# Nearest-neighbour upsampling: which block of rows each partition holds

## The chip, the core and the metric

The kernel runs on one core of a Trainium2 chip. The metric is the device time of one execution in microseconds, the median of several runs. The profile comes from one further execution, whose own time is given beside its span: the time from the first to the last instruction of the core that the profile records.

## The reference

```python
def setup_inputs():
    batch, channels, h, w = (16, 64, 64, 64)
    return {'x': np.random.randn(batch, channels, h, w).astype(np.float32), 'scale_factor': 2}

def reference(x, scale_factor):
    ...
    for i in range(new_h):
        for j in range(new_w):
            src_i = i // scale_factor
            src_j = j // scale_factor
            result[:, :, i, j] = x[:, :, src_i, src_j].copy()
```

Each of 1024 images of 64 x 64 float32 values becomes 128 x 128: every value is repeated twice along its row, and every row twice. 16.78 MB are read and 67.11 MB written.

## The kernel before

The images are taken as 65,536 rows of 64 values (256 B). The rows are cut into 128 blocks of 512 rows, so a block is 128 KiB of `x` and 512 KiB of the output, and partition p of the on-chip memory holds block p (the views `xp` and `op`, lines 173 to 176). In both views the partition is the first dimension and a partition's rows follow one another in DRAM.

One tile, `mem`, holds everything: in each partition a free area of 79 expanded rows first, and then the 512 input rows (`xt`). An expanded row is one input row in its four-fold form, 256 values or 1 KiB.

**Loads.** Line 195 issues four transfers on SyncE (SP), for the rows 0 to 32, 32 to 256, 256 to 480 and 480 to 512 of every partition: 8,192 B, 57,344 B, 57,344 B and 8,192 B per partition. A finalizer, `begin_before_barrier`, moves their issue ahead of the program's opening barrier.

**Groups.** The 512 rows are worked in nine groups of 52, 40, 52, 63, 52, 64, 63, 63 and 63 rows (`rows`, line 181). For each group VectorE (DVE) copies nine sixteenths of the rows with every value and every row repeated (line 215), ScalarE (ACT) the rest (line 216), and SP issues one store of the whole group (line 217): per partition one run of 1 KiB per row, from 40,960 to 65,536 B. Groups with even numbers are expanded into the free area at the tile's start, those with odd numbers into the place just before the end of the input rows that they use up, so the space of two groups is in use at a time. A copy into the free area waits for the store that last read it.

**Order.** All 13 transfers are issued by SP and so stand in one queue in the order of the program. The first store also waits for the third load (the manual dependency of line 219). Of the end, `close_early` makes only what has to wait for the last store wait for it.

A transfer is moved by 16 DMA engines, each of which takes the rows of 8 of the 128 partitions, one packet for a partition's row of bytes, and writes a 4 B semaphore packet behind them: 13 x (128 + 16) = 1872 packets in all.

Of the kernel before, what the change touches and what calls it, by code (L numbers as in the profile page):

```python
# [153 lines left out]
@with_exitstack  # L154
def kernel(
    ctx: ExitStack,
    tc: tile.TileContext,
    x: bass.AP,
    scale_factor: int,
    out: bass.AP,  # L160
):
    nc = tc.nc
    nc.at_finalize(begin_before_barrier)
    nc.at_finalize(close_early)
    P = nc.NUM_PARTITIONS
    s = int(scale_factor)
    B, C, H, W = x.shape
    R = B * C * H // P
    fdt = x.dtype

    xp = x.rearrange("b c h w -> (b c h) w").rearrange("(p r) w -> p r w", p=P)
    op = out.rearrange("b c (h hd) w -> (b c h) (hd w)", hd=s).rearrange(
        "(p r) w -> p r w", p=P
    )

    rows = [52, 40, 52, 63, 52, 64, 63, 63, 63]
    GROW = s * s
    FREE = 79
    WF = FREE * GROW * W
    assert sum(rows) == R
    mem_pool = ctx.enter_context(tc.tile_pool(name="mem", bufs=1))
    mem = mem_pool.tile([P, WF + R * W], fdt, name="mem")
    xt = mem[:, WF:].rearrange("p (r w) -> p r w", r=R)

    HEAD = 32
    cuts = [0, HEAD, R // 2, R - 32, R]
    loads = [
        nc.sync.dma_start(out=xt[:, lo:hi], in_=xp[:, lo:hi])  # L195
        for lo, hi in zip(cuts, cuts[1:])
    ]

    def expanded(r0, r1):
        return (  # L200
            xt[:, r0:r1].unsqueeze(2).unsqueeze(4).to_broadcast([P, r1 - r0, s, W, s])
        )

    r0 = 0
    before = (0, 0)
    for n, k in enumerate(rows):
        size = k * GROW * W
        at = 0 if n % 2 == 0 else WF + r0 * W - size
        assert at >= before[1] or at + size <= before[0]
        before = (at, at + size)  # L210
        u = mem[:, at : at + size].rearrange(
            "p (k a w b) -> p k a w b", k=k, a=s, w=W
        )
        kv = k * 9 // 16
        nc.vector.tensor_copy(out=u[:, :kv], in_=expanded(r0, r0 + kv))  # L215
        nc.scalar.copy(out=u[:, kv:], in_=expanded(r0 + kv, r0 + k))  # L216
        store = nc.sync.dma_start(out=op[:, r0 : r0 + k, :], in_=u)  # L217
        if n == 0:
            tc.add_manual_dep(
                store.ins,  # L220
                loads[-2].ins.name,
                mybir.DependencyInfo(
                    mybir.DependencyClass.Sync, mybir.DependencyReason.DATA
                ),
                reason="stores begin as the loads end",
            )
        r0 += k
# [35 lines left out]
```

## Time and profile before

| | |
|---|---|
| median of 3 runs | 197.2 us (196.95 to 197.35) |
| the profiled execution's own time | 197.0 us |
| its span | 195.7 us |
| DVE busy | 69.7 us (36%), 9 copies, the longest 9.49 us |
| ACT busy | 51.4 us (26%), 9 copies and a table load |
| DMA queue: share of 16 engines' span | 99.3% |
| moved | 83.89 MB, 429 GB/s over the span |
| a load from issue to landing | 4.6 us (the first) to 39.7 us |
| a store from issue to landing | 18.2 to 29.9 us |

A transfer is in a queue from its issue on, so its time to landing holds the time in which earlier transfers of the queue move. The profile's line of DMA tenths cuts the span in 40 slices and gives the busy share of the 16 engines in each, 9 for 90% or more; the line of GB/s gives what they moved, booked where packets end. In the chain of work that ended last, each piece is what released the next one. The trace also records every DMA packet with its size, its start and how long it took, though not which partition or which address it belongs to.

### The profile page before, as it was taken

Reading aid. Unit: us, or ns where it says so; the run is one execution under the profiler, and the core shown is the slowest. Engines: PE = TensorE matmul, PEld = TensorE weight load, DVE = VectorE, ACT = ScalarE, POOL = GpSimd, SP = SyncE. Lnnn points to the kernel's source line nnn. Section 1 sums busy time; section 2 is a strip of 40 time slices with the busy share of each in tenths; the row PEclk is TensorE's granted clock in tenths of the full one; section 3 lists DMA queues with packets and bytes.
Section 4 is the critical chain, followed back from the end, with each engine's and each line's share of the span. In section 5 each row is a group of like instructions: output and inputs, shape, how many; then the busy total and the mean of one; then the engine's idle time right before and its main releaser. Section 6 shows DMA issues by size and latency. Waiting matters only on the chain.

```text
span 195.7 us, 105 instructions
## 1 busy us (share of the span) xinstructions
DVE 69.7 (36%) x9; ACT 51.4 (26%) x10; POOL 0.2 (0%) x4
## 2 busy tenths in 40 slices
DVE  0950600000039299069008205930692079100000
ACT  0000595000036093064910006666000074000000
POOL 0000000000000000000000000000000000000000
DMA  9899889799899989899999899999999999999994
GB/s 402 375 481 457 375 375 563 310 440 523 348 442 452 526 348 512 359 422 422 422 422 523 348 523 429 429 429 429 422 422 422 422 422 422 528 514 422 435 422 211
DMA packets 1872, 83.89 MB, mean 429 GB/s; under 512 B 208, under 2 KB 208, under 8 KB 208
## 3 DMA queue, kind: packets, MB, share of 16 engines
q1 hardware_dynamic: 1872, 83.89, 99.3%
HBM read 16.78 MB, written 67.11 MB: 429 GB/s over the span
## 4 chain that ended last, share of the span: by engine, by line
DMA 67%; DVE 18%; SPq 0%; issue 0%; DVEq 0%
DMA out_dram<-mem 48%; DMA mem<-in_x_dram 19%; DVE mem L215 18%; SPq L195 0%; DVEq L215 0%; SPq L217 0%
## 5 line engine op out<-in xcount | busy, mean ns | idle before, releaser
L215 DVE COPY mem<-mem 128x8960 f32<-128x8960 f32 (+3 forms) x9 | 69.7, 7740 | 97.5 <-DMA out_dram<-mem 83.9
L216 ACT COPY mem<-mem 128x7168 f32<-128x7168 f32 (+2 forms) x9 | 50.1, 5572 | 90.8 <-DMA out_dram<-mem 84.3
L216 ACT ACT_TABLE_LOAD x1 | 1.3, 1283 | 21.6 <-DMA mem<-in_x_dram 21.6
L244 POOL MEMSET const-bfloat16-1.0<- 128x1 bf16 x1 | 0.1, 102 | 0.0
L244 POOL MEMSET const-uint8-127<- 128x1 uint8 x1 | 0.1, 102 | 0.0
L244 POOL MEMSET const-float32-0.0<- 128x1 f32 x1 | 0.1, 99 | 0.2 <-issue 0.2
L244 POOL MEMSET const-float32-1.0<- 128x1 f32 x1 | 0.1, 99 | 0.0
## 6 DMA issues: line engine op xcount, KB each, us to landing
out_dram<-mem SPq DMA_DIRECT2D x4, 8064.0 KB, 28.4
out_dram<-mem SPq DMA_DIRECT2D x3, 6656.0 KB, 19.7
mem<-in_x_dram SPq DMA_DIRECT2D x2, 7168.0 KB, 29.3
out_dram<-mem SPq DMA_DIRECT2D x1, 5120.0 KB, 29.8
mem<-in_x_dram SPq DMA_DIRECT2D x2, 1024.0 KB, 22.1
out_dram<-mem SPq DMA_DIRECT2D x1, 29.9
```

The lines of the kernel that those rows point to most:

```text
L215: nc.vector.tensor_copy(out=u[:, :kv], in_=expanded(r0, r0 + kv))
L216: nc.scalar.copy(out=u[:, kv:], in_=expanded(r0 + kv, r0 + k))
L244: nc = _bacc.Bacc("TRN2", target_bir_lowering=False, num_devices=1)
```

## The change

The view of DRAM is cut in another order. With q from 0 to 7 and a from 0 to 15, partition 8a + q now holds block 16q + a of `x` and of the output, where partition p held block p. Partitions 0 to 7 thus hold the blocks 0, 16, 32, ..., 112, partitions 8 to 15 the blocks 1, 17, 33, ..., 113, and so on. On the DRAM side each of the 13 transfers has the dimensions 16 x 8 x rows x width instead of 128 x rows x width; the tile's side stays 128 partitions. Copies, groups, waits and the order of the queue are as before.

```diff
-    xp = x.rearrange("b c h w -> (b c h) w").rearrange("(p r) w -> p r w", p=P)
+    A = 16
+    xp = x.rearrange("b c h w -> (b c h) w").rearrange(
+        "(q a r) w -> a q r w", a=A, q=P // A
+    )
     op = out.rearrange("b c (h hd) w -> (b c h) (hd w)", hd=s).rearrange(
-        "(p r) w -> p r w", p=P
+        "(q a r) w -> a q r w", a=A, q=P // A
     )
...
-        nc.sync.dma_start(out=xt[:, lo:hi], in_=xp[:, lo:hi])
+        nc.sync.dma_start(out=xt[:, lo:hi], in_=xp[:, :, lo:hi])
...
-        store = nc.sync.dma_start(out=op[:, r0 : r0 + k, :], in_=u)
+        store = nc.sync.dma_start(out=op[:, :, r0 : r0 + k, :], in_=u)
```

## The prediction

> **What bounds the kernel now.** I read the page first (busy shares, slices, the queue), then the chain of work that ended last, the busy time by stretches, and at last the trace's records of single DMA packets, which give each packet's size and time.
>
> From the page of the kernel before, the span, the busy shares, the DMA's slices in tenths and in GB/s, and the queue's totals:
>
> ```profile
> span 195.7 us, 105 instructions
> ...
> DVE 69.7 (36%) x9; ACT 51.4 (26%) x10; POOL 0.2 (0%) x4
> ...
> DMA  9899889799899989899999899999999999999994
> GB/s 402 375 481 457 375 375 563 310 440 523 348 442 452 526 348 512 359 422 422 422 422 523 348 523 429 429 429 429 422 422 422 422 422 422 528 514 422 435 422 211
> DMA packets 1872, 83.89 MB, mean 429 GB/s; under 512 B 208, under 2 KB 208, under 8 KB 208
> ...
> q1 hardware_dynamic: 1872, 83.89, 99.3%
> ```
>
> The last line is the one that counts: the packets took 99.3% of what 16 engines have in the span. DVE and ACT are busy 36% and 26%. From the chain that ended last, some of its pieces (start, length, what):
>
> ```profile
> 0.91 37.52 DMA mem<-in_x_dram
> ...
> 38.52 18.23 DMA out_dram<-mem
> ...
> 56.85 7.90 DVE mem L215
> ...
> 64.83 19.72 DMA out_dram<-mem
> ```
>
> The 7.90 us of DVE in that chain hide nothing: during them an earlier store moves, as the stretches show (length, busy time of each engine, clock, DMA share, GB/s):
>
> ```profile
> 5.00:38.00 33.00, 10.57 (x2) 10.41 (x3) 0.00 (x0) 1.00 0.97 421
> 38.00:57.00 19.00, 0.15 (x1) 0.22 (x1) 0.00 (x0) 1.00 1.02 442
> 57.00:100.00 43.00, 25.11 (x3) 22.30 (x4) 0.00 (x0) 1.00 1.00 433
> 100.00:195.70 95.70, 33.42 (x4) 18.49 (x3) 0.00 (x0) 1.00 0.99 429
> ```
>
> Loads alone (421) and stores alone (429) run at one rate. The packet records say why: on every engine a packet starts where the one before ended. A packet of 57,344 B takes 2.116 us (27.10 GB/s), 53,248 B 1.966, 40,960 B 1.514, 64,512 B 2.380, 65,536 B 2.418, and 8,192 B 0.309, with hardly a deviation in either direction of transfer. An engine takes 8 packets of each of the 13 transfers: 8 x (2 x 0.309 + 2 x 2.116 + 3 x 1.966 + 1.514 + 4 x 2.380 + 2.418) = 193.6 us, and 13 semaphore packets of 9 ns make it 193.7. Before it lie 1.0 us to the first packet and about 0.5 of slow first packets (the first 16 took 0.50 to 0.97 instead of 0.309), behind it 0.4 to the end: 195.7 in sum up to rounding. The profiled execution took 197.0, so 1.3 lie outside the span; the median of the runs is 197.2. So time is the sum of packet times on one engine, and nothing else.
>
> **The change, part by part.** It removes no instruction and adds none. The 18 copies of lines 215 and 216 work on the same partitions and columns, the waits stay, and 128 rows of the same length still go in each transfer: the same 1872 packets and 83.89 MB. What moves is which block of DRAM a partition holds, and so the form of the DRAM side of all 13 transfers: 16 x 8 rows instead of 128.
>
> *Issue.* A load's issue took SP 0.383 to 0.632 us, a store's 0.332. If the second dimension costs anything, I bound it by these rows: from 0.332 to 0.632 for the first issue, -0.05 to +0.25. Only that one has no cover. The others have the queue's earlier packets in front of them; the tightest, the store issued at 64.8 us, is ahead of the previous store's landing at 68.5 by 3.7. I take 0.
>
> *The memory's side.* Consecutive blocks are 128 KiB apart in x and 512 KiB in out. Before, neighbouring partitions were one block apart; afterwards 16, while partitions 8 apart are one block apart. The rate is set by the engine (27.10 GB/s at every size), so a better address order can only give back the 0.5 us of slow first packets. On the bad side the nearest row is those same packets: the first 16 averaged 0.73 us, 2.35 times 0.309. I take 0, because they fall on an idle queue's first touch, and keep both ends: -0.5, and 193.6 x 1.35 = +261 us.
>
> [...]
>
> *The engines' shares.* This is where I expect the cost. Before, both sides of a transfer are 128 rows, and any deal of eight rows to each engine was open. Now the DRAM side's outermost dimension is 16, as many as the engines, and the plain deal is one a per engine: engine a takes the eight neighbouring partitions 8a to 8a+7, in that order. The trace shows 16 engines filled to 99.3% at one rate, whatever the size and direction. That looks like 16 ways of fixed width, each held by one engine, and none is spare: a deal in which two engines meet on one way leaves another empty. The trace of before has no packet that shares, so I bound it. Below: the packet stays at 2.116 us, +0. (A gain is excluded: the way is full.) Above: two on one way take twice as long, 4.232 us, and the 193.6 become 387.2.
>
> I take the upper end: the rows nearest to it are those that show no slack in any packet, and the engines move in step. They ended the first transfer between 3.98 and 4.22 us and the last between 194.87 and 195.28, so 0.24 to 0.41 apart, against 8.5 us for four large packets. If two engines meet on one way for four packets and on the next way for the other four, whoever is ahead by d moves alone for d in each four, and keeps its lead where the way is shared evenly. 26 fours with d = 0.2 save 5.2 us. Sum: 387.2 + 0.1 - 5.2 = 382.1; with 1.0 + 0.5 + 0.4 around it 384.0, and 1.3 outside the span: **385.3 us**. With d = 0 it is 390.5, with 0.4 380.1.
>
> [...]
>
> **Cover.** With packets twice as long, the copies (9.5 us at most) lie beside stores of twice the length: the 3.7 us of lead grows. So nothing is added there.
>
> **Rivals.**
> 1. *The two engines get out of step.* If the shared way favours one engine, its lead grows until the two are always on different ways, and the rate of before returns. With a lead of a share f of a four, the time is 197 + 193.6 x (1 - f). If one gets 52% of the way, a four adds (0.52 - 0.48) / 0.52 = 7.7% of what is missing, f is 0.56 on average over 26 fours, and the time is 197 + 193.6 x 0.44 = 282 us. For it: a small inequality is enough. Against: no row shows one; each packet size takes the same time on all 16 engines. Range 198 to 380.
> 2. *The packets stay as they are* (not slower). This decides if the new deal, whatever it is, still gives each engine a way of its own, or if the 27.10 GB/s is the engine's own and the ways are wider. Then every packet keeps its time, and the end is 197.0 us; if the neighbouring blocks also take away the slow first packets, 0.5 less, 196.5. For it: no row shows two engines in each other's way. The change then does nothing that it could have done, the queue being 99.3% full.
> 3. *The memory is worse than that:* every packet as slow as the first ones, 197 + 261 = 458 us. Only the first packets speak for it.
>
> **How the numbers follow.** Doubled and in step (380 to 391): 0.42, the forecast, 385. Out of step (198 to 380): 0.33. Packets unchanged: 0.21, of which 0.09 with the start's 0.5 us given back. Worse than double: 0.04. A measurement of this kernel tells about 0.2% (0.4 us) from no change. So faster 0.09, same 0.12, slower 0.42 + 0.33 + 0.04 = 0.79. Without the unchanged case 0.25 would be left out, so the range reaches down to it, less the 0.5 and a little spread: 196.3 to 391. The likeliest case's own range is 380 to 391.
>
> **What will show it.** Doubled: packets of 57,344 B near 4.2 us, the slices near 215 GB/s, the queue's share still near 99%, the first large loads landing near 77 us instead of 38, DVE and ACT copies at their old 9.49 and 6.16 us. Out of step: packet times between 2.1 and 4.2 and a rate that rises along the span. Unchanged: 2.116 us and 429 GB/s. If the loads alone or the stores alone change, the share of ways is not the cause, since it would meet both; a memory cause may differ between them. I am wrong if the packets keep 2.1 us, or if the queue's share falls, which would mean waiting for issues or copies that I count as hidden.

## The result and the profile after

The changed kernel takes 362.1 us (median of 4 runs, 359.0 to 362.6) against 197.1, a ratio of 1.833 (95% interval 1.829 to 1.837). The profiled execution took 359.0, with a span of 357.7. Here and below, executions more than 1.5% above a kernel's fastest are left out of times and ratios; only run 4 has any, two of its four.

The page of the changed kernel, the same lines as shown of before (span, busy shares, the DMA's slices in tenths and in GB/s, packets, queue share):

```profile
span 357.7 us, 105 instructions
...
DVE 69.7 (19%) x9; ACT 51.4 (14%) x10; POOL 0.2 (0%) x4
...
DMA  9999999999899999999998999999999999999940
GB/s 220 205 205 205 205 205 205 205 213 293 197 220 234 229 255 226 256 219 256 260 238 229 257 262 293 224 279 256 275 253 267 260 281 289 260 281 274 238 137 14
DMA packets 1872, 83.89 MB, mean 235 GB/s; under 512 B 208, under 2 KB 208, under 8 KB 208
...
q1 hardware_dynamic: 1872, 83.89, 96.1%
```

The same packets and bytes, engines that are full up to the tail, and little more than half the rate: each packet takes longer, and nobody waits for an issue. The GB/s line has two parts. In its first eight slices, the loads, it stands at 205 after a first 220. In the stores it climbs from about 220 to 280, and then falls off at the end.

The chain that ended last, the pieces that answer to those of before (start, length, what):

```profile
77.96 34.43 DMA out_dram<-mem
...
112.48 7.90 DVE mem L218
...
120.46 45.34 DMA out_dram<-mem
```

The same copy of 7.90 us is there; the store that took 18.23 us takes 34.43. By stretches (length, busy time, clock, DMA share, GB/s):

```profile
38.00:74.00 36.00, 3.10 (x1) 10.41 (x3) 0.00 (x0) 1.00 0.98 204
...
200.00:335.00 135.00, 33.42 (x4) 18.49 (x3) 0.00 (x0) 1.00 1.00 266
335.00:357.00 22.00, 0.00 (x0) 0.00 (x0) 0.00 (x0) 1.00 0.38 109
```

The last line is the tail: the engines ended between 336.5 and 357.3 us, 20.8 us apart, where they had ended 0.4 apart before. On average they ended 12.2 us before the last one, 3.4% of the span; that is the fall of the queue's share from 99.3% to 96.1%. The packet records show the rest. A packet of 57,344 B in the loads takes 4.20 to 4.49 us (mean 4.41, it was 2.116), every one of the 256. A packet of 64,512 B in the stores takes from 2.38 to 5.27 (mean 3.89, it was 2.380). Joined end to start, the packets of the third store (53,248 B, 1.966 us before) run on two of the engines like this (us):

```
ahead:   1.97 4.00 4.15 4.38   1.97 3.66 4.15 4.38
behind:  3.89 4.15 4.16 2.35   3.92 4.15 4.15 2.05
```

The times repeat with a period of four packets. That fits the forecast's picture: an engine that is ahead has the first packet of each four for itself, one that is behind the last. The trace doesn't say which two engines are partners.

### The profile page after: what moved, and what is told of

It reads as the page before. It is cut to its first block, busy times and chain, and to the rows that moved or that the text cites. A ratio compares the mean times of both kernels' runs of the same rounds, so it can differ in the third digit from the quotient of the medians.

```text
span 357.7 us, 105 instructions
## 1 busy us (share of the span) xinstructions
DVE 69.7 (19%) x9; ACT 51.4 (14%) x10; POOL 0.2 (0%) x4
## 3 DMA queue, kind: packets, MB, share of 16 engines
q1 hardware_dynamic: 1872, 83.89, 96.1%
## 4 chain that ended last, share of the span: by engine, by line
another core or an unknown queue 50%; DMA 22%; DVE 12%; issue 0%; DVEq 0%; SPq 0%
DMA out_dram<-mem 22%; DVE mem L218 12%; DVEq L218 0%; SPq L220 0%
```

## The experiments

The theory was that of the forecast: 16 as the outermost dimension deals eight neighbouring partitions to each engine, so two engines meet on one way into the tile for four packets and on the next for four (a way is, in this theory, a path to a group of partitions, and a lead is how far one of the two engines is ahead of the other). That a way serves four packets in turn, and that the engines that meet stand four apart, as the expectations of the later runs have it, were assumptions of mine; no trace of before shows either. The rivals: the address order in DRAM, the two-dimensional form as such, and, for the pace of the stores, that leads play no part. Runs 8 to 12 were executed once each; in them fewer of the loads, one to three instead of four, are issued ahead of the opening barrier (`EARLY`, which the extracts leave out).

**1. The same change with 32 instead of 16.**

```diff
-    A = 16
+    A = 32
```

> The map of the change with 32 in place of 16 as the outermost dimension: partition 4a + q holds block 32q + a (a from 0 to 31, q from 0 to 3). Neighbouring partitions are now 32 blocks apart in DRAM, and the form is still two-dimensional; but an engine's share of two values of a can be any two groups of four partitions. If the deal is the cause (eight neighbouring partitions to an engine because 16 is outermost), groups of four can be dealt as before, every packet is back at 2.12 us for 57,344 B and the time at 197 us (196.3 to 198). If the address order in DRAM is the cause, it is at least as far from the order of before as the change's: 300 us or more. If it is the two-dimensional form as such, 360 us.

198.0 us against 197.6, ratio 1.0023 (1.0014 to 1.0033). Two stretches of it, one in the loads and one in the stores:

```profile
5.00:38.00 33.00, 10.98 (x2) 10.41 (x3) 0.00 (x0) 1.00 0.96 417
100.00:195.00 95.00, 33.42 (x4) 18.49 (x3) 0.00 (x0) 1.00 1.00 432
```

The rate of before is back, with neighbouring partitions 32 blocks apart (16 MiB in the output) and a two-dimensional form. So neither neighbours far apart in DRAM nor the form costs the time as such. What is left, 0.43 us, is the first issue: the first packet starts at 1.44 us, where it started at 1.02.

**2. The block map of before in halves of 64 partitions.**

```diff
-        nc.sync.dma_start(out=xt[:, lo:hi], in_=xp[:, lo:hi])
+        nc.sync.dma_start(out=xt[a:b, lo:hi], in_=xp[a:b, lo:hi])
         for lo, hi in zip(cuts, cuts[1:])
+        for a, b in ((0, 64), (64, 128))
```

The stores are cut in the same way.

> The kernel before with its block map and its one-dimensional form, each transfer cut into two: partitions 0 to 63, then 64 to 127. Addresses in DRAM and the amount per packet stay. If ways into the tile belong to groups of partitions, half the partitions reach only half of the ways and each way has two engines for the whole transfer: packets near 4.4 us for 57,344 B, 340 to 410 us depending on how far engines get ahead into the next half. If addresses or the two-dimensional form are the cause, 197 to 200 us: 13 more issues of 0.5 us are hidden.

361.1 us, ratio 1.827 (1.820 to 1.835): the change's time with addresses and form of before. Its loads and its stores:

```profile
5.00:75.00 70.00, 10.98 (x2) 10.41 (x3) 0.00 (x0) 1.00 1.03 213
85.00:340.00 255.00, 58.67 (x7) 41.02 (x7) 0.00 (x0) 1.00 1.00 249
```

Which partitions the 16 engines reach at one time decides: with 64 neighbouring ones the loads move at 213 GB/s and the stores at 249, where the kernel before has 421 and 429 with all 128.

**3. and 4. The change in the loads alone, and in the stores alone.** Against the change, the one has

```diff
-        store = nc.sync.dma_start(out=op[:, :, r0 : r0 + k, :], in_=u)
+        store = nc.sync.dma_start(out=op[:, r0 : r0 + k, :], in_=u)
```

with the old view `op`, and the other

```diff
-        nc.sync.dma_start(out=xt[:, lo:hi], in_=xp[:, :, lo:hi])
+        nc.sync.dma_start(out=xt[:, lo:hi], in_=xp[:, lo:hi])
```

with the old view `xp`.

> The new block map for the loads alone; the stores keep the map of before, so the output's blocks of rows are in another order than the reference's. Parts add up if loads and stores are slowed by the same cause independently: the third load landed at 38.1 us before and at 77.0 us with the change, so 197.1 + 38.9 = 236 us (234 to 238), with stores at 2.38 us per packet of 64,512 B. If the slow loads only shift a waiting time, less.

238.0 us, ratio 1.206 (1.203 to 1.209). The loads run at the change's pace, the stores at the old one:

```profile
5.00:75.00 70.00, 10.98 (x2) 10.41 (x3) 0.00 (x0) 1.00 1.00 211
85.00:235.00 150.00, 58.68 (x7) 41.02 (x7) 0.00 (x0) 1.00 0.99 430
```

> The new block map for the stores alone; the loads keep the map of before, so the output's blocks of rows are in another order than the reference's. By addition 362.1 - 38.9 = 323 us (318 to 340); packets of the stores start near twice their time and vary more from store to store as engines get out of step, as in the change.

313.4 us (the median of 312.3 and 314.6), ratio 1.589 (1.583 to 1.595), 4.6 us under the range. Here it is the other way round, and the stores gain on the way:

```profile
5.00:38.00 33.00, 10.59 (x2) 10.41 (x3) 0.00 (x0) 1.00 0.97 421
45.00:65.00 20.00, 0.00 (x0) 0.00 (x0) 0.00 (x0) 1.00 0.96 210
65.00:310.00 245.00, 58.68 (x7) 41.02 (x7) 0.00 (x0) 1.00 0.96 250
```

The excesses are 40.9 and 116.3 us, 157.1 in sum, against 165.0 for both together. So loads and stores are each slowed, and nearly independently. The large loads of run 3 are at about twice their time throughout (4.37 us for 57,344 B on average); in run 4 the engines end 3.0 us apart in the first store and 19.1 in the last.

**5. One store at a time**, to take the leads away: each store is issued when the one before has landed.

```diff
+        else:
+            tc.add_manual_dep(store.ins, previous.ins.name, ...)
+        previous = store
```

> The change, each store issued only when the one before has landed, so that all engines begin every store together. If the engines of a pair gain in the change because one gets ahead of the other from store to store, this takes the gain away: packets near 2.1 times their old time in every store, 8 x 19.35 us x 2.11 = 327 us for the stores, 81 us for the loads and nine gaps of 2 to 3 us: 420 to 440 us. If leads play no part, the stores keep the change's pace and only the gaps are added: 362 + 20 = 382 us.

417.5 us, ratio 2.117 (2.114 to 2.120), 2.5 us under the range. The stores, gaps included, no longer climb above the loads' rate:

```profile
5.00:74.00 69.00, 10.98 (x2) 10.41 (x3) 0.00 (x0) 1.00 1.03 215
85.00:410.00 325.00, 58.67 (x7) 41.02 (x7) 0.00 (x0) 1.00 0.94 199
```

The engines end each store 1.4 us apart, and the packets of a store cost an engine 314.7 us in all. In the change it is 263.7, in the kernel before 154.8: factors of 2.03 and 1.70. The remaining 20 us are the gaps. So the leads of the change save it 51 us of packets, on average over the engines.

**6. A change of way after every packet.** The block map of the change, each transfer cut into four.

```diff
-        nc.sync.dma_start(out=xt[:, lo:hi], in_=xp[:, :, lo:hi])
+        nc.sync.dma_start(out=xt[c:P:4, lo:hi], in_=xp[:, c : P // A : 4, lo:hi])
         for lo, hi in zip(cuts, cuts[1:])
+        for c in range(4)
```

> The block map of the change, each transfer cut into four by the partition modulo 4: the partitions c, c + 4, c + 8 and so on. An engine now takes partitions 8a + c and 8a + c + 4 one after the other, so by the theory of shared ways it changes its way after every packet instead of after four, and a lead of one packet (2 us) is enough to be out of step. Shared ways: loads still near 4.4 us per large packet if leads do not grow there, stores near 2.0 to 2.5 us after the first ones; 235 to 300 us. Address order as the cause: 360 us. Price of 39 more issues: 39 x 0.5 us, hidden behind the queue.

260.2 us, ratio 1.316 (1.314 to 1.319). The loads and the stores:

```profile
5.00:73.00 68.00, 0.00 (x0) 0.00 (x0) 0.00 (x0) 1.00 1.00 216
100.00:255.00 155.00, 58.68 (x7) 41.02 (x7) 0.00 (x0) 1.00 0.99 408
```

With the addresses and the deal of the change, the stores are nearly back at full rate: 64,512 B take 2.41 us on average. That fits the theory, by which a lead of one packet suffices here; the leads themselves were not measured. The loads keep 4.22 us per large packet. Between loads and stores there is a difference that the theory didn't have. Some 10 of the 260 us are a gap: the last load ends at 78.0 us and the first store's packets start at 87.8, since the copies here began only at 78.6, behind the loads.

**7. Another address order, with the form and the deal of before.** Each group of rows is one contiguous stretch of DRAM.

```diff
+            in_=xf[P * lo : P * hi].rearrange("(p r) w -> p r w", p=P),
...
+        ... out=of[P * r0 : P * (r0 + k)].rearrange("(p r) w -> p r w", p=P)
```

> The kernel before with another address order and the one-dimensional form: for each of the nine groups of rows the 128 partitions hold one contiguous stretch of x and of the output (partition pitch 10 to 16 KB in x and 40 to 64 KB in the output instead of 128 KiB and 512 KiB); the loads are cut at the groups, nine instead of four. If the address order costs nothing while every engine has its own way, the packets keep their time: 197 us (196.3 to 198.5). If the order in DRAM matters by itself, it shows here as packets other than 2.38 us for 64,512 B.

198.7 us, ratio 1.0075 (1.006 to 1.009), just over the range. The packets of the stores keep their times (64,512 B: 2.380). The 1.5 us lie in the nine shorter loads: 13,312 B took 0.525 us on average where most took 0.498, 16,128 B 0.626 instead of 0.601, and the engines end 1.0 us apart. The stores:

```profile
45.00:195.00 150.00, 58.68 (x7) 41.02 (x7) 0.00 (x0) 1.00 1.01 436
```

**8. Four engines held back in the loads.**

```diff
+        if lo == 0:
+            nc.sync.dma_start(
+                out=xt[4:8, R // 2 : R - 32], in_=xp[0, 4:8, R // 2 : R - 32]
+            )
```

> The change, with one more transfer behind the first load: 57,344 B for each of the four partitions 4 to 7, which a later load writes again with the same values. With an outermost dimension of 4 it should run on four engines alone and hold them back by about 8.5 to 9 us, the time of four large packets. If engines meet in pairs four engines apart, on ways that change after four packets, then four of these pairs are brought out of step: in the two large loads eight engines have packets near 2.12 us and the other eight near 4.46 us, for 128 of 256 packets each. The time stays within 345 to 375, since the other pairs end last. If the address order is the cause, all large packets stay near 4.46 us and the time is 362 to 372.

364.9 us; the time is in the range, the reading isn't. Four engines did run the extra transfer (eight packets more than in the change, four of them of data) and stayed a packet behind, but no large packet came below 3.9 us. Either the loads aren't slow because of pairs, or the pairs still in step hold back all the others. While the extra transfer ran, all 16 engines had a packet of 7.1 to 7.9 us, which speaks for the second.

**9. Is a crowded way felt by all?** The kernel before, with a load and a store of partitions 4 to 7 alone.

```diff
+            nc.sync.dma_start(
+                out=mem[4:8, :N].rearrange("p (r w) -> p r w", w=W), in_=xp[4:8, :224]
+            )
...
+            nc.sync.dma_start(out=op[4:8, R - 40 :, :], in_=u[4:8])
```

> The kernel before with two small transfers for partitions 4 to 7 alone: a load of 57,344 B each behind the second load, and a store of 40,960 B each behind the second store, both overwritten later. Four engines then meet at four neighbouring partitions while the others move what they always move. If a crowded way holds back only those who use it, four or five engines have packets of about 4 x 2.1 us and the others keep 2.12 us. If a crowded way holds back all engines in a load, all sixteen have a packet of 5 us or more there. In the store I expect the others to keep their time, since packets of 2.38 us stood beside packets of 5 us in the stores of the change. Time 200 to 215 us.

211.2 us. Stretches before and at the extra load, and at the extra store:

```profile
10.00:21.00 11.00, 0.00 (x0) 0.00 (x0) 0.00 (x0) 1.00 0.96 417
21.00:31.00 10.00, 0.54 (x1) 0.55 (x1) 0.00 (x0) 1.00 1.04 184
...
76.00:82.00 6.00, 0.00 (x0) 0.00 (x0) 0.00 (x0) 1.00 1.14 418
```

In the load all sixteen packets that started around 21 us took 6.7 to 7.4 us, and the next sixteen 3.0 to 3.9, though the extra load is only four packets: the rate falls to 184. In the store the four packets of 40,960 B took 5.5 to 5.7 us (1.51 alone), and the others kept 1.97 beside them: 418. So in this run the extra load held back every engine, and the extra store only its own four packets.

**10. Leads in all pairs, first try.** Six extra loads behind the first one.

```diff
+            for i in range(3):
+                nc.sync.dma_start(
+                    out=mem[64 + i : 80 + i : 4, :N], in_=xb[64 + i : 80 + i : 4, :N]
+                )
+            for i in range(3):
+                nc.sync.dma_start(
+                    out=mem[i : 48 + i : 4, :N], in_=xb[i : 48 + i : 4, :N]
+                )
```

> The change, with six more loads behind the first one, whose values are overwritten later: three with an outermost dimension of 4 and three with 12, each 57,344 B per partition and with neighbouring rows four partitions apart, so that they do not all end on one way. If the lowest-numbered engines run them, engines 0 to 3 fall six packets behind, 4 to 11 three, 12 to 15 none: in every pair four engines apart one is three packets ahead of the other. If engines meet in such pairs, and a single pair in step is what held all the others back in the earlier run with one such transfer, most packets of the two large loads should now fall below 3.5 us, with some at 2.12. If loads are slowed by something other than pairs, the large packets stay at 4.2 to 4.5 us. Time: 340 to 375 in the one case, 375 to 395 in the other.

384.0 us, and it tells nothing of the question: all three later loads waited for the extra ones after all, and so the engines began the large loads together and kept 3.8 to 4.6 us per packet in them. The queue's issues show it, line 201 being the loads':

```profile
0.00 0.68 SPq L201 DMA_DIRECT2D mem<-in_x_dram  x1
...
25.20 1.90 SPq L201 DMA_DIRECT2D mem<-in_x_dram  x3
```

**11. Leads in all pairs, second try**, on neighbouring partitions, with which the second large load doesn't wait.

```diff
+            for i in range(3):
+                a = 64 + 4 * i
+                nc.sync.dma_start(out=mem[a : a + 4, :N], in_=xb[a : a + 4, :N])
+            for i in range(3):
+                a = 12 * i
+                nc.sync.dma_start(out=mem[a : a + 12, :N], in_=xb[a : a + 12, :N])
```

> The change, with six more loads behind the first one, overwritten later: three for four partitions (64 to 75 in all) and three for twelve (0 to 35 in all), 65,024 B per partition. Unlike in the run before, the second large load no longer waits for them, so the leads should last. Engines 0 to 3 then fall six such packets behind, 4 to 11 three, 12 to 15 none, and in each pair four engines apart one is 3.4 of its 57,344 B packets ahead. The six loads themselves crowd a few ways and cost 30 to 50 us. If loads are slow because pairs of engines move in step over shared ways, packets in the second large load now reach 2.12 us, with a median below 3.5. If they stay between 4.2 and 4.5 us in spite of the leads, it isn't the pairs' step that makes the loads slow. Time: 350 to 385 in the one case, 390 to 420 in the other.

398.8 us, which is in the range that I had given for the other case: the extra loads cost more than I had allowed (packets of up to 11.2 us until 67 us). The packets answer the question. Once the extra loads are over, the large loads run in turn fast and slow:

```profile
72.00:76.00 4.00, 4.00 (x1) 0.00 (x0) 0.00 (x0) 1.00 0.93 401
78.00:82.00 4.00, 0.00 (x0) 0.00 (x0) 0.00 (x0) 1.00 0.96 229
84.00:87.00 3.00, 0.00 (x0) 0.00 (x0) 0.00 (x0) 1.00 0.88 382
89.00:93.00 4.00, 1.82 (x1) 1.74 (x2) 0.00 (x0) 1.00 0.96 229
```

Of the 144 large packets that start between 67 and 94 us, 56 take under 2.2 us, and the median is 2.53. All engines are fast at the same time, and slow at the same time (the 27 packets that start from 83.3 to 87 us: 2.12 to 2.13; the six that start from 89.5 to 90.5: 4.16 to 4.19). That is what 3.4 packets of lead in a period of four should give, if everybody is held back while any pair shares. By the expectation's count, each pair then shares for 0.6 packets of every four, and the pairs among engines 0 to 7 and among 8 to 15 do so at different times, since the latter are 3.4 packets ahead of the former. With everyone at half pace for both, four packets should take (4 + 2 x 0.6) x 2.116 = 11.0 us. The pattern recurs after 11.1: packets of 2.29 us, the first ones of a slow stretch, start at 76.1 and at 87.2 us.

**12. Leads of eight engines over the other eight.** Three extra loads of 8 partitions take the place of the six.

```diff
+            for i in range(3):
+                a = 8 * i
+                nc.sync.dma_start(out=mem[a : a + 8, :N], in_=xb[a : a + 8, :N])
```

> The run before with three extra loads of eight partitions each (0 to 23 in all, 65,024 B each, overwritten later) in place of its six. If they run on the eight lowest engines, engines 0 to 7 fall three packets behind 8 to 15, while engines four apart stay level. If the pairs are four apart (0 and 4, 1 and 5, and so on), no pair gets a lead: once the extra loads are over, the large packets are back at 4.2 to 4.5 us and none comes near 2.12 us. If the pairs are eight apart, or if any lead among the engines relieves the loads, packets of 2.12 us appear as in the run before. Time: 375 to 400 with pairs four apart, 350 to 385 otherwise.

383.7 us, in the range for pairs four apart. Its stretches after the extra loads:

```profile
40.00:60.00 20.00, 2.89 (x1) 0.00 (x0) 0.00 (x0) 1.00 1.08 224
60.00:84.00 24.00, 3.09 (x1) 10.41 (x3) 0.00 (x0) 1.00 0.95 196
```

All 216 large packets that start after 35 us take 4.27 to 4.49 us, though two groups of eight engines stand some packets apart: eight begin the last load at about 89 us, the other eight at about 104. A lead as such relieves nothing. Pairs eight apart are excluded, since all of them would have had a lead here, as in run 11. Pairs four apart fit both runs; other pairings that run 11 separates and run 12 doesn't would fit too.

## Why the prediction was right, and where not

**The bound: right.** The sum of packet times set the end in both kernels, and the copies kept their 9.49 and 6.16 us. The queue's share did fall, to 96.1%, which the prediction had named as a sign of waiting for issues or copies; it is the tail, and up to its end an engine's packets follow one another as before (343.4 us of data packets to an engine between the first start at 1.46 and the mean end at 345.1). A small slip: 27.10 GB/s doesn't hold at every size, as 8,192 B in 0.309 us are 26.5. Nothing rests on it.

**The deal of partitions: right.** Run 1 keeps the rate with 32 x 4 blocks (417 and 432 GB/s), run 2 loses it by the partitions alone (213 and 249), and with the leads of run 11 large packets of the loads take 2.12 us where in run 12 they take 4.27 to 4.49: partners out of step are relieved, if the pairs are those of the theory.

**The price of a shared packet: nearly right.** I took twice; with both in step it was 4.41 over 2.116 = 2.09 in the large loads, and 2.03 in the stores of run 5.

**The leads: wrong.** I wrote that the pair "keeps its lead where the way is shared evenly" and took 0.2 us throughout, which "save 5.2 us". No run shows the four packets to a way, on which the 26 fours of that sum rest; what the change shows in their place is packet times that repeat with a period of four, on two engines in the third store. In the loads the lead was kept, at another size: the ends of a transfer lay 0.89 us apart in the first and 0.88 in the last. In the stores the spread grew to 20.8 us. An engine's packets came to 79.7 us in the loads and 263.7 in the stores, 343.4 in all instead of 382.1. That is 38.7 less, of which the slowest engine, which sets the end, gives back 12.4, nearly all of it the 12.2 by which it lags behind the mean. The 26.3 us that remain are the difference between the 384.0 of my sum and the span of 357.7 (the 0.5 of slow first packets, which the 343.4 contain, and the 0.4 more of issue cancel). So the likeliest case's own range, 380 to 391, missed: the loads went by it, the stores by rival 1 (198 to 380), which holds the 362.1. The wide range of 196.3 to 391 would have held rivals 1 and 2 alike, so that it holds the result says little for the forecast. Run 5, which takes the stores' leads away, is slower than the change by 55 us, its gaps included.

**The issue: undersized.** I bounded the first one by +0.25 us and took 0. It took 0.672 us instead of 0.383, +0.29, and the first packet came 0.44 later. The issue of a store went from 0.332 to 0.538 us, hidden as expected.

**The memory's side: right to take 0.** Runs 1 and 7 keep the rate with other address orders (432 and 436 GB/s in the stores), run 2 loses it with the old one (249), and in run 11 packets with the change's own addresses take 2.12 us. A wide pitch as such cost no rate: in run 1 neighbouring partitions lie 4 MiB apart in `x` and 16 MiB in the output, and move at 417 and 432 GB/s.

**Open:** why the leads grow in the stores. That all engines are held to one pace in loads (6.7 to 7.4 us for all sixteen in run 9) would keep leads from growing there; what makes the engine ahead gain in stores was not measured. Why the load onto four partitions holds back all engines, at 184 GB/s, is open as well. Which engine has which partitions stands in no trace; the deal and the pairs are inferred from the runs.

## What to carry to other kernels

Read the time of single DMA packets: where it doubles while the queue stays full (here 4.41 us for 2.116, at a DMA share of 0.98), look at which engines meet at which partitions. Look at the form of a transfer's DRAM side too: here an outermost dimension of 16 doubled the packets in the loads, and one of 32, with addresses spread even wider, took 198.0 us against 197.6, the difference being the first packet's later start. Before a transfer touches a part of the partitions only, test what its crowding costs the others: in run 9 such a load was paid by everything else that loaded, at 184 GB/s instead of 417.

## What the runs showed of the hardware that was not expected

- A load onto four neighbouring partitions by four engines held back all sixteen (6.7 to 7.4 us for packets of 2.12), a store from them only its own four packets (5.5 to 5.7 us for 1.51; run 9).
- In the large loads of the change, which the theory has in step, a packet took 2.09 times its time before, not 2 (4.41 us over 2.116); the stores of run 5 took 2.03 times theirs (314.7 us over 154.8).
- In the stores of the change the engines drifted apart by themselves, from 1.1 us at the end of the first store to 20.8 at the end of the last, and gained by it (263.7 us of packets to an engine, against 314.7 in run 5); with each transfer cut into four (run 6) the stores came back to 408 GB/s.
- With a two-dimensional DRAM side the first packet came 0.39 to 0.44 us later than the 1.02 us of before (runs 1 and 3 and the change), with loads in the old form it didn't (run 4: 1.01 us). The form isn't the only thing that delays it: in run 2, with the old form and 64 partitions, it came at 1.36 us.
